# The third block product of the MLP's second matmul as seven inner products, and the order of the products around it

## The chip, the cores and the metric

The kernel runs on one core of a Trainium2 chip. The metric is the device time of one execution, in microseconds (us). The engines are TensorE (PE, with PEld for its weight loads), VectorE (DVE), ScalarE (ACT), GpSimd (POOL) and SyncE (SP), which issues most of the loads.

## The reference

One layer of a transformer-like block on 1024 tokens of width 1024. The part that matters here is the end of it, the MLP with a squared ReLU, and the gated residual behind it:

```python
def _sq_relu_mlp(h, w1, w2):
    return jnp.square(jax.nn.relu(h @ w1)) @ w2

y_x = _sq_relu_mlp(_modulate(x, g_pre_mlp[l], sh2, sc2), w_mlp_in[l], w_mlp_out[l])
x = x + gt2 * _rmsnorm(y_x, g_post_mlp[l])
```

`w1` is 1024 x 4096 and `w2` is 4096 x 1024, all in float32. The second product is therefore (1024 x 4096) times (4096 x 1024).

## The kernel before

**Precision.** Every large matrix is split in a high part `h` (rounded, by ACT, line 169) and a low part `l` (what is left, by DVE, line 175). One float32 product is three matmuls: high times high, high times low, low times high (`three`, lines 221 to 223). A matmul takes 128 x 128 weights and up to 512 columns, and adds into one of eight PSUM banks of 512 columns.

**Seven products instead of eight.** The second product is cut into 2 x 2 blocks (512 tokens, 2048 of the inner dimension, 512 columns) and is computed in the way of Strassen and Winograd, with seven block products P1 to P7 and sums of blocks. The left blocks are the hidden values A11, A12, A22 and their sums S1 to S4, which the first product leaves in DRAM (`hidd`; `keep`, line 1876). The right blocks are columns of `w2` (b11, b12, b21, b22), with the differences t1, t2, t3, t4 made on DVE (`operands`, lines 2037 to 2061). Banks named `pyx`, `pyy`, `pyv` and `pyz`, four each (one for every 128 tokens), take the sums. P1 and P2 go into x (the first block of the result). P6 + P1 gives u2. P7 + u2 goes into the row halves of tokens 512 to 1023, with P5 added, then P4 into v, and P3 and P5 into z.

**Groups.** A product has eight groups (`NG`). A group is 256 of the inner dimension: four banks, each with two steps of three matmuls, so 24 matmuls of 512 columns. The order of the groups is written out by hand in `items`:

- P1, eight groups
- P6 and P2 alternating, then P7 and P5 alternating
- P4 and P3 alternating for four groups, then P3's last four, then P4's last four

`prepare` takes the next item of that list: it issues its loads on SP, its differences and low parts on DVE and its high parts on ACT. It is called ahead of each group, for the item three places on (`AHEAD`). The order of instructions on PE, ACT, DVE and SP is the order of the program in this part (`in_order`), so that an instruction which waits holds up all that are behind it on its engine. Buffers also set the pace: `wraw` has four raw pages (loads of `w2`), `h` four pages (loads of hidden values), `whl` four pairs of high and low parts, and the common pool 33 pages. The weights' high part of an item can only be written when the group four places before has left its pair.

**The tail.** P3's last two groups and P4's last four are computed bank by bank, so that a bank of 128 tokens is done early. Behind each finished bank come the row steps. `gated` takes the mean square on ACT (line 154) and multiplies by the gate on DVE (line 2154). `rsqrt_of` forms the sum of both halves on DVE (line 161) and the root on POOL (line 163). `end` adds the residual (`xo`, line 2162) and stores the row tile. The last 128 tokens are computed in two halves of 256 columns (banks `pyv` and `pyw`). Before the last four groups of P4, DVE adds u2 into the banks v (line 2231).

In the loop of P4 and P3 the four row halves of tokens 512 to 1023 get P5 (`s5`, copied out of z by ACT), are squared and are gated:

```python
c = half(4 + g, 1)
nc.vector.tensor_tensor(c, c, s5[g], add)
gated(4 + g, 1, c)
```

Of the kernel before, what the change touches and what calls it, by code (L numbers as in the profile page):

```python
# [18 lines left out]
P = 128  # L19
# [84 lines left out]
def hybrid_block(ctx, tc, x, ctx_in, w_mod, mod_pages, w_u, b_mod, gp1, gp2, w_in, pool_w, rpb, w_out, w1, w2, vectors,  # L104
# [17 lines left out]
    def page(name, dt=F32):  # L122
        return act.tile([P, 1024], dt, tag="pg", name=name)
# [145 lines left out]
    def mod_gate(name, acc, g, bank):  # L269
        nc.vector.tensor_tensor(acc[:, :256], mod_sums_of(name, acc, bank), g, mul)  # L270
# [1248 lines left out]
    with tc.tile_pool(name="ps2", bufs=6, space=PSUM) as ps2:  # L1519

      def bank(name):
          if name[:3] == "phv" or name in ("poz_0", "poz_1") or name[:2] in ("px", "py") and name[-2:] in ("_3", "_7"):
              return lasting(name)
          return ps2.tile([P, 512], F32, tag="mm", name=name)

      with ExitStack() as tmp2:
# [257 lines left out]
        def second_steps(b12, b22):  # L1784
# [13 lines left out]
            for name in ("T2", "T1", "T3", "B22", "T4"):  # L1798
# [6 lines left out]
        EARLY, SPILLED = 10, 6  # L1805

        hidd = {n: [dram.tile([P, 1024], F32, tag=f"hd{n}_{g}", name=f"hd{n}_{g}") for g in range(NPAIR // 2)]
                for n in ("A11", "A12", "A22", "S1", "S2", "S3", "S4")}

        s1d = [dram.tile([P, 512], F32, tag=f"s1_{p}", name=f"s1_{p}") for p in range(SPILLED)]  # L1810

# [44 lines left out]
            nc.scalar.activation(r, r, AF.Square)  # L1856

        def kept(name, p):
            return hidd[name][p // 2][:, (p % 2) * 512 : (p % 2) * 512 + 512]


# [149 lines left out]


        w2v = w2.rearrange("(k i p) n -> i p k n", i=2, p=P)
        t1, t2 = {}, {}
# [5 lines left out]
        def wcols(name, i, h, g):  # L2020
            return columns(wraw.tile([P, 1024], F32, tag="raw", name=f"{name}_{g}"), i, h, g)
# [6 lines left out]
        def hidden(name, g, early=False):  # L2028
            if early:
                r = wraw.tile([P, 1024], F32, tag="raw", name=f"hr{name}_{g}")  # L2030
            else:
                r = tmp.tile([P, 1024], F32, tag="h", name=f"hr{name}_{g}", bufs=4)
            nc.sync.dma_start(r, hidd[name][g])
            return split_pages(f"hh{name}_{g}", r)


        def operands(name, g, made=None):
            made = made or high_low
            if name == "P1":
                t1[g] = columns(page(f"b11_{g}"), 0, 0, g)  # L2040
                return hidden("A11", g, g <= AHEAD + 1), made(f"b11_{g}", t1[g])
            if name == "P2":
                return hidden("A12", g), made(f"b21_{g}", wcols("b21", 1, 0, g))
            if name == "P6":

                b12, b22 = wcols("b12", 0, 1, g), wcols("b22", 1, 1, g)
                nc.vector.tensor_tensor(t1[g], b12, t1[g], sub)
                t2[g] = page(f"t2_{g}")
                nc.vector.tensor_tensor(t2[g], b22, t1[g], sub)
                return hidden("S2", g), made(f"t2_{g}", t2[g])  # L2050
            if name == "P5":
                return hidden("S1", g), made(f"t1_{g}", t1[g])
            if name == "P7":
                b12, b22 = wcols("b12", 0, 1, g), wcols("b22", 1, 1, g)
                nc.vector.tensor_tensor(b12, b22, b12, sub)
# [4 lines left out]
            nc.vector.tensor_tensor(b21, b21, t2[g], sub)  # L2060
# [54 lines left out]
        with tc.issue_after(first[ET.PE]), in_order(ET.PE, ET.Activation, ET.DVE, ET.SP):  # L2115
# [5 lines left out]
            def four(name):  # L2121
                return [bank(f"{name}_{t}") for t in range(4)]
# [24 lines left out]
            def half(m, h):  # L2147
                return rows[m][:, h * 512 : (h + 1) * 512]
# [31 lines left out]


            pg = bank("pgb")
            x = four("pyx")
            for g in range(NG):
                if g == 1:
                    gain = mod_gain(gp2, page("gpb")[:, :256], nc.gpsimd)
                if g == 3:
                    mod_gate("b", acc_b[-1], gain, lambda name: pg)
                    mod_out("b", acc_b[-1])
                group(x, "P1", g)  # L2190
            s1 = halves("s1")
            for t in range(4):
                nc.scalar.copy(s1[t], x[t])
            y = four("pyy")
            for g in range(NG):
                group(y, "P6", g)
                if g == NG // 2:
                    G2 = gate_page("b")
                if g == NG - 1:
                    u2 = halves("u2")  # L2200
                    for t in range(4):
                        nc.vector.tensor_tensor(u2[t], y[t], s1[t], add)
                group(x, "P2", g, more=True)
            for t in range(4):
                rows[t] = page(f"row{t}")
                gated(t, 0, x[t])
            v, z = four("pyv"), four("pyz")
            for g in range(NG):
                group(v, "P7", g)
                if g == NG - 1:  # L2210
                    for t in range(4):
                        rows[4 + t] = page(f"row{4 + t}")
                        nc.vector.tensor_tensor(half(4 + t, 1), v[t], u2[t], add)
                group(z, "P5", g)
            s5 = halves("s5")
            for t in range(4):
                nc.scalar.copy(s5[t], z[t])
            for g in range(NG // 2):
                group(v, "P4", g, more=True, last=(g == NG // 2 - 1))
                group(z, "P3", g, more=True)  # L2220
                c = half(4 + g, 1)
                nc.vector.tensor_tensor(c, c, s5[g], add)
                gated(4 + g, 1, c)
            for g in range(NG // 2, NG - 2):
                group(z, "P3", g, more=True)
            while coming:
                prepare()

# [71 lines left out]
```

## Time and profile before

| what | value |
|---|---|
| median of 3 runs | 1021.81 us (1021.76 to 1022.08) |
| profiled execution: span from first to last instruction | 1019.4 us |
| mean granted clock of TensorE | 0.998 |
| busy over the span | PE 99%, DVE 73%, ACT 54%, POOL 15% |
| first matmul of the second product | 707.8 us |
| last matmul | 1013.42 us |

The profile gives the span of its execution, and no time of it beside that; the median of the runs is 2.4 us longer. Times within the profile are us from the start of the span. A row in order of time reads: start, length, engine, line, operation, what is written from what is read, and in brackets how long the engine had been idle and what it had waited for. Names leave out buffer numbers, so that the four banks of `pyv` all read `pyv`. Matmuls are pipelined: the distance from one start to the next is their rate, and their length is not.

### The profile page before, as it was taken

What the parts mean: (1) busy time and instruction counts of PE and PEld (TensorE: products, weight loads), DVE (VectorE), ACT (ScalarE), POOL (GpSimd) and SP (SyncE); (2) the same over time, 40 slices, a digit from 0 to 9 for tenths busy, and PEclk for the clock granted to TensorE, in tenths of its full rate; (3) what the DMA queues carried; (4) which work ended last, traced back from release to release, by engine and by line L of the source; (5) the groups of instructions that cost most, each with busy time, mean ns of one, the idle gap of its engine ahead of it and who ended that gap; (6) DMA issues with size and microseconds to landing.
All of it is one profiled execution on the core that took longest, in us unless ns stands there. A gap on an engine that the chain in (4) does not pass through costs nothing.

```text
span 1019.4 us, 16277 instructions
## 1 busy us (share of the span) xinstructions
PE 1008.7 (99%) x6010; PEld 834.4 (82%) x6010; DVE 746.4 (73%) x1170; ACT 548.1 (54%) x964; POOL 154.5 (15%) x234
## 2 busy tenths in 40 slices
PE   8999999999999999999999999999999999999997
PEld 5788888878998888888888888888888888888886
DVE  5588767977885689879988888745757666557576
ACT  6672254348986746786555544555543343334442
POOL 4111210166774221410000000000000000000002
PEclk9999999999999999999999999999999999999999
DMA  9899798641448945885776657537967766556555
GB/s 368 314 295 305 256 265 293 206 104 43 96 95 204 232 183 187 297 216 197 256 260 208 213 194 225 177 135 251 347 218 261 248 228 214 200 167 203 169 184 226
DMA packets 117312, 222.72 MB, mean 218 GB/s; under 512 B 9521, under 2 KB 47281, under 8 KB 117233
## 3 DMA queue, kind: packets, MB, share of 16 engines
q1 hardware_dynamic: 90736, 171.14, 50.0%
q0 software_dynamic: 9360, 19.58, 9.3%
q10 hardware_dynamic: 17136, 30.97, 8.1%
q8 instruction: 47, 0.77, 0.3%
q14 instruction: 33, 0.26, 0.1%
HBM read 168.16 MB, written 52.45 MB: 216 GB/s over the span
## 4 chain that ended last, share of the span: by engine, by line
PE 96%; DMA 2%; DVE 1%; ACT 0%; issue 0%; SPq 0%; DVEq 0%; ACTq 0%
PE pu L476 4%; PE pa L1288 4%; PE S L1208 3%; PE phx L221 3%; PE phz L221 3%; PE phv L221 3%; PE pyx L221 3%; PE phx L223 3%; PE phx L222 3%; PE phv L223 3%; PE pyx L222 3%; PE pyz L221 3%; PE phz L223 3%; PE phv L222 3%; PE phz L222 3%; PE pyz L222 3%
## 5 line engine op out<-in xcount | busy, mean ns | idle before, releaser
L1234 ACT ACTIVATE sp<-sp,nm 128x640 f32<-128x640 f32 (+1 forms) x64 | 51.4, 802 | 10.9 <-DVE ri L1238 5.1
L1223 DVE CUSTOM_DVE_ANT_0 sp<-S,tab 128x640 f32<-128x640 f32 (+1 forms) x56 | 44.5, 795 | 13.9 <-PE pz L1254 9.5
L1855 ACT ACTIVATE c<-c 128x512 f32<-128x512 f32 x48 | 30.3, 632 | 44.8 <-DVE c L1975 25.6
L169 ACT CAST wpS<-S 128x512 fp32r<-128x512 f32 x64 | 38.7, 616 | 27.4 <-PE phv L223 9.7
L221 PE MATMUL phx<-thB,wpA 128*128 128x512 f32 x128 | 50.2, 392 | 0.0
L222 PE MATMUL phx<-tlB,wpA 128*128 128x512 f32 x128 | 49.8, 389 | 0.0
L223 PE MATMUL phx<-thB,wpA 128*128 128x512 f32 x128 | 49.8, 389 | 0.0
L175 DVE TENSOR_TENSOR wpS<-S,wpS 128x512 fp32r<-128x512 f32 x64 | 43.5, 688 | 7.6 <-ACT wpS L169 7.5
L163 POOL TENSOR_TENSOR ry<-vy,nhalf 128x1 f32<-128x1 f32 x7 | 5.4, 767 | 275.6 <-DVE vy L161 275.6
L1856 ACT ACTIVATE c<-c 128x512 f32<-128x512 f32 x48 | 30.3, 631 | 15.1 <-DVE sa L1938 12.1
L221 PEld LDWEIGHTS phx<-thB,wpA 128*128 128x128 f32 x128 | 24.0, 188 | 5.5 <-ACT s L1906 0.4
L223 PEld LDWEIGHTS phx<-thB,wpA 128*128 128x128 f32 x128 | 24.0, 188 | 5.0
L222 PEld LDWEIGHTS phx<-tlB,wpA 128*128 128x128 f32 x128 | 24.0, 188 | 4.9
L1273 DVE COPY pt<-T 128x512 f32<-128x512 f32 x32 | 22.0, 687 | 5.5 <-PE T L1254 5.5
L1288 PE MATMUL pa<-pt,v 128*64 128x128 f32 x352 | 25.9, 279 | 0.2
L221 PE MATMUL phv<-thT,wpA 128*128 128x512 f32 x64 | 25.0, 391 | 0.0
L221 PE MATMUL phz<-thB,wpS 128*128 128x512 f32 x64 | 25.0, 391 | 0.0
L223 PE MATMUL phv<-thT,wpA 128*128 128x512 f32 x64 | 24.9, 389 | 0.0
L222 PE MATMUL phz<-tlB,wpS 128*128 128x512 f32 x64 | 24.9, 389 | 0.0
L222 PE MATMUL phv<-tlT,wpA 128*128 128x512 f32 x64 | 24.9, 389 | 0.0
L221 PE MATMUL phy<-thT,wpS 128*128 128x512 f32 x64 | 24.9, 389 | 0.0
L222 PE MATMUL phy<-tlT,wpS 128*128 128x512 f32 x64 | 24.9, 389 | 0.0
(1179 smaller groups left out, 3442.6 us busy)
## 6 DMA issues: line engine op xcount, KB each, us to landing
b<-in_w SPq DMA_DIRECT2D x64, 512.0 KB, 4.3
hrS<-hdS SPq DMA_DIRECT2D x32, 512.0 KB, 5.1
hrA<-hdA SPq DMA_DIRECT2D x24, 512.0 KB, 5.6
wm<-in_mod_pages SPq DMA_DIRECT2D x16, 512.0 KB, 9.3
wa_0w<-in_w SPq DMA_DIRECT2D x16, 512.0 KB, 5.0
wa_1w<-in_w SPq DMA_DIRECT2D x16, 512.0 KB, 4.3
hdA<-c ACTq DMA_DIRECT2D x32, 256.0 KB, 2.2
hdS<-sa ACTq DMA_DIRECT2D x32, 256.0 KB, 2.2
```

What stands on the lines that cost most here:

```text
L169: nc.scalar.copy(hi, src)
L175: nc.vector.tensor_tensor(lo, src, hi.bitcast(F32), sub)
L221: nc.tensor.matmul(ps, ahi, bhi, start=first, stop=False, skip_group_check=more)
L222: nc.tensor.matmul(ps, ahi, blo, start=False, stop=False, skip_group_check=more)
L223: nc.tensor.matmul(ps, alo, bhi, start=False, stop=last, skip_group_check=more)
L476: nc.tensor.matmul(pus[b][j], wk(wgt, k, low, j * P, P), r, start=(k == 0 and n == 0), stop=(k == KT - 1 and n == 2))
L1208: nc.tensor.matmul(S[e][:, c0 : c0 + k[0].shape[1]], q[n_q][hs, cols], k[n_k][hs], start=(n_q + n_k == 0), stop=(n_q == 1))
L1223: nc.vector.tensor_tensor_reduce(out=to, in0=s, in1=bt, scale=1.0, scalar=BIG, op0=add, op1=ALU.min, accum_out=nm)
L1234: nc.scalar.activation(sp, sp, AF.Exp, bias=least[i, e], scale=-1.0, accum_out=sums[i][:, e : e + 1])
L1288: nc.tensor.matmul(pa[e * HD : (e + 1) * HD, cols], v[:, f : f + HD], turns[i][:, e, c] if c < 4 else fifths[i][:, :, (e + 1) * HD : (e + ...
L1855: nc.scalar.activation(r, src, AF.Relu)
L1856: nc.scalar.activation(r, r, AF.Square)
```

## The change

P3 (S4 times b22) is itself cut into 2 x 2 blocks and computed with seven inner products M1 to M7 of 256 tokens, 1024 of the inner dimension and 256 columns. Each has two halves (h = 0, 1) of 24 matmuls of 256 columns. One half stands ahead of each group of P1 (from the fifth) and P2 (two ahead of P2's first and fifth). S4 is kept in a tensor of its own, `hidq`, from which pieces of 256 columns are loaded. The inner sums are read from banks `pyi...`, which alternate between the two lasting banks, and are put together in four pages; those that hold the result get u2 in the loop of P4 and P5, and are added in the tail (`u4`) in the place of u2.

The order of the other products becomes: P1 and P2 with the inner ones, P6 with P7, P4 with P5, P5's last four, P4's last four. P7 takes t3 from P6's preparation and loads nothing of `w2`. P4 makes t2 anew from b22 and t1, with one more load and one more subtraction. P5 goes into z alone, so that the row halves of tokens 512 to 1023 get it in the tail.

```diff
-          if name[:3] == "phv" or name in ("poz_0", "poz_1") or name[:2] in ("px", "py") and name[-2:] in ("_3", "_7"):
+          if (name[:3] in ("phv", "pyi") or name in ("poz_0", "poz_1") or name[:2] == "px" and name[-2:] in ("_3", "_7")
+                  or name in ("pyy_3", "pyv_3", "pyz_3")):
               return lasting(name)
...
+        hidq = [dram.tile([P, 4, 1024], F32, tag=f"hq{h}", name=f"hq{h}") for h in range(2)]
...
             if name == "P6":
                 b12, b22 = wcols("b12", 0, 1, g), wcols("b22", 1, 1, g)
                 nc.vector.tensor_tensor(t1[g], b12, t1[g], sub)
-                t2[g] = page(f"t2_{g}")
-                nc.vector.tensor_tensor(t2[g], b22, t1[g], sub)
+                nc.vector.tensor_tensor(b12, b22, b12, sub)
+                t3[g] = b12
+                nc.vector.tensor_tensor(b22, b22, t1[g], sub)
...
             if name == "P7":
-                b12, b22 = wcols("b12", 0, 1, g), wcols("b22", 1, 1, g)
-                nc.vector.tensor_tensor(b12, b22, b12, sub)
-                return hidden("S3", g), made(f"t3_{g}", b12)
+                return hidden("S3", g), made(f"t3_{g}", t3.pop(g))
-            if name == "P3":
-                return hidden("S4", g), made(f"b22_{g}", wcols("b22", 1, 1, g))
-            b21 = wcols("b21", 1, 0, g)
-            nc.vector.tensor_tensor(b21, b21, t2[g], sub)
+            b22, b21 = wcols("b22", 1, 1, g), wcols("b21", 1, 0, g)
+            nc.vector.tensor_tensor(b22, b22, t1[g], sub)
+            nc.vector.tensor_tensor(b21, b21, b22, sub)
             return hidden("A22", g), made(f"t4_{g}", b21)
...
+        INNER = ("M1", "M5", "M6", "M4", "M2", "M3", "M7")
+        def inner_operands(name, h):
+            a = lambda r, c, at=None: inner_raw(f"a{r}{c}{name}_{h}", True, r, c, h, at)
+            b = lambda r, c, at=None: inner_raw(f"b{r}{c}{name}_{h}", False, r, c, h, at)
+            new = lambda n: kept_raw.setdefault((n, h), page(f"{n}i_{h}"))
+            if name == "M1":
+                x, y = a(0, 0, new("S")), b(0, 0, new("T"))
+            elif name == "M5":
+                x, more, y, less = a(1, 0, new("S1")), a(1, 1), kept_raw["T", h], b(0, 1)
+                combine(x, x, more, add)
+                combine(y, less, y, sub)
...
+            else:
+                x, z, y, less = a(0, 0), a(1, 0), b(1, 1), b(0, 1)
+                combine(x, x, z, sub)
+                combine(y, y, less, sub)
+            return split_pages(f"hh{name}_{h}", x), high_low(f"w{name}_{h}", y)
...
-        items = [("P1", g) for g in range(NG)]
-        for a, b in (("P6", "P2"), ("P7", "P5")):
-            items += [(n, g) for g in range(NG) for n in (a, b)]
-        items += [(n, g) for g in range(NG // 2) for n in ("P4", "P3")] + [("P3", g) for g in range(NG // 2, NG)]
+        inner = iter([(n, h) for n in INNER for h in range(2)])
+        items = [("P1", g) for g in range(4)]
+        for n in [("P1", g) for g in range(4, NG)] + [("P2", g) for g in range(NG)]:
+            items += [*islice(inner, 2 if n in (("P2", 0), ("P2", 4)) else 1), n]
+        items += [(n, g) for g in range(NG) for n in ("P6", "P7")]
+        items += [(n, g) for g in range(NG // 2) for n in ("P4", "P5")] + [("P5", g) for g in range(NG // 2, NG)]
         items += [("P4", g) for g in range(NG // 2, NG)]
...
+            def inner_group(name, h):
+                prepare()
+                a, w = made.pop((name, h))
+                if h == 0:
+                    inner_banks[name] = bank(f"pyi{name}")
+                ps = inner_banks[name]
+                for t in range(2):
+                    for j in range(4):
+                        ts, cs = slice(j * 256 + t * P, j * 256 + (t + 1) * P), slice(j * 256, (j + 1) * 256)
+                        three(ps[:, t * 256 : (t + 1) * 256], a[0][:, ts], a[1][:, ts], w[0][:, cs], w[1][:, cs],
+                              h + t + j == 0, h == 1 and j == 3, more=t > 0)
+                if h == 1:
+                    inner_kept(name, ps)
...
+                group(v, "P7", g)
             for t in range(4):
+                rows[4 + t] = page(f"row{4 + t}")
+                nc.vector.tensor_tensor(half(4 + t, 1), v[t], u2[t], add)
+            z = four("pyz")
+            u4 = [inner_part(f"c{t // 2}")[:, t % 2 * 512 : t % 2 * 512 + 512] for t in range(4)]
             for g in range(NG // 2):
                 group(v, "P4", g, more=True, last=(g == NG // 2 - 1))
-                group(z, "P3", g, more=True)
-                c = half(4 + g, 1)
-                nc.vector.tensor_tensor(c, c, s5[g], add)
-                gated(4 + g, 1, c)
+                group(z, "P5", g)
+                nc.vector.tensor_tensor(u4[g], u4[g], u2[g], add)
...
             for t in range(4):
-                token_sums(z, t, [made["P3", g] for g in (NG - 2, NG - 1)], False, True, True)
-                finish(t, 1, z[t], xts[t], u2[t])
+                token_sums(z, t, [made["P5", g] for g in (NG - 2, NG - 1)], False, True, False)
+                c = half(4 + t, 1)
+                nc.vector.tensor_tensor(c, c, z[t], add)
+                gated(4 + t, 1, c)
+                finish(t, 1, z[t], xts[t], u4[t])
```

More of the change, by code (lines that the diff above doesn't have):

```diff
@@ L2047, in operands @@
                 nc.vector.tensor_tensor(t1[g], b12, t1[g], sub)
-                t2[g] = page(f"t2_{g}")
-                nc.vector.tensor_tensor(t2[g], b22, t1[g], sub)
-                return hidden("S2", g), made(f"t2_{g}", t2[g])
+                nc.vector.tensor_tensor(b12, b22, b12, sub)
+                t3[g] = b12
+                nc.vector.tensor_tensor(b22, b22, t1[g], sub)
+                return hidden("S2", g), made(f"t2_{g}", b22)
             if name == "P5":
@@ L2182, in hybrid_block @@
             pg = bank("pgb")
-            x = four("pyx")
[L2184 to L2191, printed above, removed]
+            inner_banks, parts = {}, {}
+            by_two = lambda v: v.rearrange("p (t n) -> p t n", t=2)
@@ new lines, in hybrid_block @@
+            x = four("pyx")
+            for name, g in items[: items.index(("P6", 0))]:
+                if name in INNER:
+                    inner_group(name, g)
+                elif name == "P1":
+                    if g == 1:
+                        gain = mod_gain(gp2, page("gpb")[:, :256], nc.gpsimd)
+                    if g == 3:
+                        mod_gate("b", acc_b[-1], gain, lambda name: pg)
+                        mod_out("b", acc_b[-1])
+                    group(x, "P1", g)
+                    if g == NG - 1:
+                        s1 = halves("s1")
+                        for t in range(4):
+                            nc.scalar.copy(s1[t], x[t])
+                else:
+                    group(x, "P2", g, more=True)
+                    if g == NG // 2:
+                        G2 = gate_page("b")
@@ L2192, in hybrid_block @@
             for t in range(4):
-                nc.scalar.copy(s1[t], x[t])
-            y = four("pyy")
+                rows[t] = page(f"row{t}")
+                gated(t, 0, x[t])
+            y, v = four("pyy"), four("pyv")
             for g in range(NG):
                 group(y, "P6", g)
-                if g == NG // 2:
-                    G2 = gate_page("b")
                 if g == NG - 1:
```

69 lines of the change are left out of this document (52 added, 17 removed).

## The prediction, made before the changed kernel was run

> **What bounds the kernel now.** I read the page first, then a table of the stages of the second MLP product, then single instructions in order of time on TensorE and VectorE.
>
> ```profile
> span 1019.4 us, 16277 instructions
> PE 1008.7 (99%) x6010; PEld 834.4 (82%) x6010; DVE 746.4 (73%) x1170; ACT 548.1 (54%) x964; POOL 154.5 (15%) x234
> ...
> 751.90:838.90 87.00, 87.00 (x385) 72.06 (x384) 57.67 (x52) 34.38 (x39) 0.00 (x0) 1.00 0.71 240
> 926.00:969.50 43.50, 43.50 (x194) 36.02 (x193) 27.12 (x27) 20.29 (x26) 0.00 (x0) 1.00 0.65 205
> 969.50:991.25 21.75, 21.75 (x98) 18.01 (x97) 17.26 (x17) 9.05 (x9) 0.00 (x0) 1.00 0.44 150
> 991.25:1013.70 22.45, 22.45 (x122) 19.40 (x120) 17.58 (x30) 6.81 (x18) 5.37 (x7) 1.00 0.70 278
> 1013.70:1019.40 5.70, 0.00 (x0) 0.00 (x0) 2.04 (x5) 0.77 (x3) 0.00 (x0) 0.69 0.26 92
> ```
>
> The columns of the stages are the stretch, its length, and the busy time of PE, PEld, DVE, ACT and POOL. TensorE (PE) is busy without a gap to 1013.7, at a granted clock of 1.00. So before 1013.7 a saving counts only if it takes time from PE, and new work elsewhere counts only if PE, or the end, comes to wait for it. VectorE (DVE) is the second engine: 79% busy at 969.5 to 991.25 and 78% in the last PE stage. That is where I looked for the price.
>
> **Part 1, the matmuls.** The third product was 8 groups of 24 matmuls of 512 columns, 192 in all. The seven inner ones take 7 x 2 halves x 24 = 336 matmuls of 256 columns. Both kinds stand in the last PE stage:
>
> ```profile
> 991.47 0.39 PE L221 MATMUL pyv<-t_4h,hhA_4h 128*128 128x512 f32 x1
> ...
> 1007.56 0.39 PE L223 MATMUL pyv<-t_7h,hhA_7l 128*128 128x512 f32 x1
> ...
> 1007.79 0.28 PE L221 MATMUL pyv<-t_4h,hhA_4h 128*128 128x256 f32 x1
> 1007.79 0.19 PEld L222 LDWEIGHTS pyv<-t_4l,hhA_4h 128*128 128x128 f32 x1
> ...
> 1013.42 0.28 PE L223 MATMUL pyw<-t_7h,hhA_7l 128*128 128x256 f32 x1
> ```
>
> The first pair of rows spans 72 matmuls of 512 columns: 16.09 us over 71 steps, 0.2266 each (the 0.39 is a pipelined length, not a rate). The second spans 48 of 256 columns: 5.63 over 47 steps, 0.1198 each. So 192 x 0.2266 = 43.51 goes and 336 x 0.1198 = 40.25 comes: **-3.26 us**, not the eighth (5.4) that the columns alone promise. A group of 512 lasts 24 x 0.2266 = 5.44, an inner half 2.88.
>
> The Trainium skill (TensorE: Matmul & The Clock Gate, Back-to-back issue gap) gives an isolated step of N/2.4 + 2.5 ns, so 215.8 and 109.2 ns, and the sum by it, an estimate, would be -4.8 us. The rows here are 5% and 10% slower than that, and the measured steps are kept.
>
> **Part 2, feeding the inner stage: nothing.** From the fifth group of P1 to the last of P2 lie 12 groups and 14 inner halves: 65.3 + 40.3 = 105.6 us of PE. DVE owes 26 items two low parts each (1.14 from one start to the next, rows below), 16 combinations of 1024 columns (M5 2, M6 2, M4 1, M3 1, M7 2, for both halves) at 1.25, and 7 half pages of sums at 0.60: 59.3 + 20 + 4.2 = 83.5, 79%. Items are prepared three ahead, at least 2.88 + 5.44 + 2.88 = 11.2 us before use, and an item with two combinations needs 4.8. If that cover fails, PE stops for what DVE or a load is late (rival 3). Loads: 124 of 512 KB for 120 in the whole second product (inner 28, P4 +8, P3 -16, P7 -16). All go in order on SP's queue, and pieces of 1 KB a partition have a nearest row of their own (w1's pages), beside 2 KB pieces:
>
> ```profile
> b<-in_w SPq DMA_DIRECT2D x64, 512.0 KB, 4.3
> wa_0w<-in_w SPq DMA_DIRECT2D x16, 512.0 KB, 5.0
> GB/s 368 314 295 305 256 265 293 206 104 43 96 95 204 232 183 187 297 216 197 256 260 208 213 194 225 177 135 251 347 218 261 248 228 214 200 167 203 169 184 226
> ```
>
> A landing 0.7 us later is hidden in that lead. Cost at 0; ends 0 and +4.6 (rival 3). Two inner sums share the pair of PSUM banks, and each is read out by ACT or DVE while the inner product on the other bank runs (5.8): 0. The fourth P1 sum's move to the six other banks, the stores of S4 (same pieces, other tensor) and P6/P7 (8.3 of 10.9 us on DVE for a pair of groups: three subtractions and four low parts) are 0 for the same cover.
>
> **Part 3, P4 straight behind P7.** Before, P5's last group lay between P7's last group and P4's first; now P4 adds to the very banks that DVE must read first (v + u2). The like place before is P6's end:
>
> ```profile
> 732.55 1.22 DVE L2047 TENSOR_TENSOR b<-b,b 128x1024 f32<-128x1024 f32 x1
> 733.80 1.22 DVE L2049 TENSOR_TENSOR t<-b,b 128x1024 f32<-128x1024 f32 x1
> ...
> 833.48 0.39 PE L223 MATMUL pyy<-t_7h,hhS_7l 128*128 128x512 f32 x1
> ...
> 833.91 0.69 DVE L2202 TENSOR_TENSOR u<-pyy,s 128x512 f32<-128x512 f32 x1 [0.67 <-PE pyy L223]
> 834.52 1.22 DVE L2055 TENSOR_TENSOR b<-b,b 128x1024 f32<-128x1024 f32 x1
> 835.65 1.22 DVE L175 TENSOR_TENSOR hhS_1l<-hrS,hhS_1h 128x1024 fp32r<-128x1024 f32 x1
> 836.90 1.23 DVE L175 TENSOR_TENSOR t_1l<-b,t_1h 128x1024 fp32r<-128x1024 f32 x1
> 838.04 1.88 DVE L2154 TENSOR_TENSOR row<-pyx,Gb 128x512 f32<-128x512 f32 x3
> ```
>
> P6's group ends at 833.48 + 0.23 = 833.71, and DVE then does u2's last quarter, one subtraction, two low parts, and reaches the next sum at 838.04. P4's preparation has two dependent subtractions (1.25 by the first two rows), so the first v + u2 starts at about 839.24 and ends at 839.93; PE wants that bank at 833.71 + 5.44 = 839.15. **+0.8 us** on PE; ends 0 (the preparation is ahead) and +2. Below 0 is excluded here and in part 2: PE has no gap in these stages that could close.
>
> **Part 4, the tail.** The fourth product now subtracts twice per group. P5's end, which sets the row halves of tokens 4 to 7, now comes last: their add, square and gate leave the P4/P3 loop and stand in the tail, once per tile, on DVE's queue ahead of everything that finishes rows.
>
> ```profile
> 933.87 0.69 DVE L2222 TENSOR_TENSOR row<-row,s 128x512 f32<-128x512 f32 x1
> 935.35 0.69 DVE L2154 TENSOR_TENSOR row<-row,Gb 128x512 f32<-128x512 f32 x1 [0.79 <-ACT jy L154]
> ...
> 981.69 1.23 DVE L175 TENSOR_TENSOR t_5l<-b,t_5h 128x1024 fp32r<-128x1024 f32 x1 [1.99 <-ACT t_5h L169]
> 982.83 1.22 DVE L2060 TENSOR_TENSOR b<-b,t 128x1024 f32<-128x1024 f32 x1
> ...
> 986.32 1.22 DVE L2060 TENSOR_TENSOR b<-b,t 128x1024 f32<-128x1024 f32 x1
> ...
> 989.80 2.22 DVE L2231 TENSOR_TENSOR pyv<-pyv,u 128x512 f32<-128x512 f32 x4
> 991.92 0.68 DVE L2176 TENSOR_TENSOR c<-pyz,u 128x512 f32<-128x512 f32 x1
> ...
> 993.53 0.68 DVE L2154 TENSOR_TENSOR row<-c,Gb 128x512 f32<-128x512 f32 x1
> 994.13 0.68 DVE L2176 TENSOR_TENSOR c<-pyz,u 128x512 f32<-128x512 f32 x1
> ...
> 1002.39 1.28 DVE L2162 SCALAR_TENSOR_TENSOR xo<-row,ry,xo 128x1024 f32<-128x1024 f32 x1 [0.44 <-POOL ry L163]
> ...
> 1004.47 1.28 DVE L2162 SCALAR_TENSOR_TENSOR xo<-row,ry,xo 128x1024 f32<-128x1024 f32 x1
> ...
> 1009.65 1.28 DVE L2162 SCALAR_TENSOR_TENSOR xo<-row,ry,xo 128x1024 f32<-128x1024 f32 x1
> ...
> 1011.37 0.43 DVE L2171 TENSOR_TENSOR row<-pyv,Gb 128x256 f32<-128x256 f32 x1 [0.43 <-ACT jy L154]
> ...
> 1014.83 1.54 DVE L2266 SCALAR_TENSOR_TENSOR xo<-row,inverse_y,xo 128x512 f32<-128x512 f32 x3
> ```
>
> Step by step, on the times of before. (a) The second subtraction of P4's groups 4 and 5 falls into waits (the 1.99 at 981.69). Groups 6 and 7 follow back to back (982.83, 986.32), so each adds 1.25: v + u2 starts 2.5 late, at 992.3. PE wants its first bank at 991.47 and stands about 1.6, which does not decide. (b) DVE reaches the first tile at 991.92 + 2.5 = 994.42. From 991.92 to the fourth finished row (1002.39) lay 10.47 us for four tiles, with next to no idle. Each tile now adds a sum, which waits out ACT's square before it may be overwritten (933.87 to 935.35: 1.48), and a gate of 0.60 (993.53 to 994.13): 2.08, four times 8.3. The fourth row is at 994.42 + 18.8 = 1013.2. (c) The next three rows take 2.08 each (1002.39 to 1004.47): the seventh, 1009.65 before, is at 1019.4. (d) Then the last tile's first quarter (+1.2), the small sum (+0.35), second quarter, root and reciprocal (+0.6) and three pieces of 1.54: end at 1023.2, where it was 1014.83 + 1.54 = 1016.37. PE's last matmul, at 1013.42 + 1.6, no longer ends it. **+6.8 us.** Removed in exchange: the same four sums and gates from the loop and four ACT copies, all under PE time: 0. Ends: +4.3 (a costs nothing) and +8 (the reciprocal roots on POOL, on which each row waits, take longer).
>
> **Sum.** -3.26 + 0.8 + 6.8 = +4.4 us against the span: 1019.4 to 1023.8. The median of the runs is 1021.81, 2.4 above the span, and I carry that over: **1026.2 us**, 0.4% slower. About 0.2% (2 us) is what a measurement of this kernel can tell from no change.
>
> **Rivals.** (1) *The tail's new DVE work is hidden*, and PE stays the end: 1021.81 - 3.26 + 0.8 = 1019.4. For it: in the two stages from 991.25 DVE has 4.9 and 3.7 us idle, together about the 8.3 that is added. Against it: DVE's idle time lies after 1007.8, behind the rows, and 3.7 of it after PE's end. It decides if the chain from 991.92 to the last row grows by under 2.5 us; I count 6.8, so 4.4 would have to be wrong. Chance 0.13. (2) *The tail starts on time*: P4's preparations run far enough ahead that (a) is nothing: 1026.2 - 2.5 = 1023.7, no change. For it: the waits of almost 2 us ahead of two low parts. Against it: the last two have none. 0.10. (3) *The inner stage starves*: M7 needs 4 loads a half beside 2 for each group, 6 x 0.524 MB in 8.32 us, 378 GB/s, where the page's best slice is 368 and the best late one 347. Two such rounds at 297 GB/s would take 21.2 us instead of 16.6: up to +4.6, so 1028 to 1031. Against it: the halves of M2 and M3 ahead load one page each, and buffers take loads early. 0.12. (4) *Weight loads set the inner step*: at the 0.19 of a load, 336 x 0.188 = 63.2 us, 1026.2 + 22.9 = 1049. Against it: the 48 matmuls after 1007.79 step at 0.12 with loads of 0.19 beside them. 0.03. The Trainium skill (TensorE: Matmul & The Clock Gate, The mechanism) says that weight loads overlap matmuls in flight only when the row group differs, which speaks for (4); the trace shows overlap with full 128 x 128 weights, so here it does not hold.
>
> **How the numbers follow.** The forecast has 0.62 and a range of its own of 1024.6 (half of (a) hidden and nothing at P4: -1.25 - 0.8, with the slack of a few tenths) to 1028.5 (+2 at P4 and the tail's upper end of +8). With (2) and (3) that is 0.84 between 1022 and 1030.5, which is the range; left out are (1) and (4). Faster 0.13 is (1), within 0.2% 0.10 is (2), slower 0.77 the rest.
>
> **What would show it.** Right: inner matmuls stepping at 0.12 and no PE gap from P1 to P7; a gap near 0.8 ahead of P4's first matmul; a gap near 1.6 ahead of the last product's second half; DVE at nearly full from there to the end, PE's last matmul 8 us ahead of DVE's last instruction (3 before). Wrong: PE's last matmul followed by the final row within 3 us (1), the first row's sum at its old distance from P5's end (2), PE gaps before inner matmuls (3), steps of 0.19 (4).

## The result, and the profile after

The changed kernel takes **1027.44 us** (median of 5 runs, 1027.31 to 1027.78) beside 1021.89 for the kernel before on the same chip (5 runs, 1021.76 to 1022.08): a ratio of 1.0055 [1.0043, 1.0067], 5.55 us slower. On a second chip it was 1.0055 [1.0041, 1.0069]. The forecast was 1026.2, 4.4 slower.

First the head of the changed kernel's page with its fourth view (the engine shares of the chain of work that ended last, followed back from the last instruction), then that view of the kernel before, then the stages of the second MLP product, with the columns that the prediction explained.

```profile
span 1025.5 us, 16659 instructions
PE 1006.3 (98%) x6154; PEld 838.3 (82%) x6154; DVE 795.2 (78%) x1217; ACT 559.4 (55%) x974; POOL 154.6 (15%) x234
...
DVE 0%; POOLq 0%; DVEq 0%; ACT 0%; issue 0%; ACTq 0%
```

```profile
PE 96%; DMA 2%; DVE 1%; ACT 0%; issue 0%; SPq 0%; DVEq 0%; ACTq 0%
```

```profile
751.90:836.58 84.68, 84.68 (x499) 75.38 (x497) 70.64 (x65) 43.32 (x47) 0.00 (x0) 1.00 0.74 252
836.58:924.84 88.26, 87.44 (x386) 71.86 (x384) 71.66 (x66) 36.94 (x44) 0.00 (x0) 1.00 0.57 198
...
968.48:990.24 21.76, 21.76 (x97) 17.84 (x95) 19.16 (x17) 9.24 (x9) 0.00 (x0) 1.00 0.56 198
990.24:1014.12 23.88, 22.35 (x121) 19.33 (x120) 19.28 (x32) 9.23 (x26) 4.20 (x5) 1.00 0.50 195
1014.12:1025.50 11.38, 0.16 (x2) 0.00 (x0) 7.64 (x14) 0.92 (x5) 1.17 (x3) 0.71 0.59 230
```

PE is no longer in the chain that ends the program, as far as the view follows it: the shares are near 0 because it goes back only over the last 4.6 us, and the rows of DVE below show what lies ahead of that. The stretch behind PE's last matmul has grown from 5.7 to 11.4 us. P1 to P2 with the inner products (the first row, most of it) run without a gap in PE although DVE is 83% busy there; in the last 21.8 us before P5's end DVE is 88% busy, where it was 79%.

PE has two waits in the whole of the second product, and had none before. The view of waits of the changed kernel, for PE from 705 us on (engine, line that waits, releaser: total, times, longest):

```profile
PE pyv L221 <- DVE pyv L2319: 1.5, 1, 1.5
PE pyv L221 <- DVE row L2305: 0.8, 1, 0.8
```

PE in order of time: the first inner half (24 matmuls), the first matmul behind it, then the two gaps.

```profile
730.74 0.28 PE L221 MATMUL pyiM<-wM_0h,hhM_0h 128*128 128x256 f32 x1
...
733.49 0.28 PE L223 MATMUL pyiM<-wM_0h,hhM_0l 128*128 128x256 f32 x1
733.61 0.40 PE L221 MATMUL pyx<-b_4h,hhA_4h 128*128 128x512 f32 x1
...
923.63 0.39 PE L223 MATMUL pyv<-t_7h,hhS_7l 128*128 128x512 f32 x1
924.84 0.47 PE L221 MATMUL pyv<-t_0h,hhA_0h 128*128 128x512 f32 x1 [0.82 <-DVE row L2305]
...
990.01 0.39 PE L223 MATMUL pyz<-t_7h,hhS_7l 128*128 128x512 f32 x1
991.93 0.47 PE L221 MATMUL pyv<-t_4h,hhA_4h 128*128 128x512 f32 x1 [1.53 <-DVE pyv L2319]
```

And DVE in order of time, from the preparation of P4's last group to the end. These answer to the rows that the prediction showed of 986.32 to 1014.83.

```profile
986.35 1.22 DVE L2063 TENSOR_TENSOR b<-b,b 128x1024 f32<-128x1024 f32 x1
987.60 1.23 DVE L2064 TENSOR_TENSOR b<-b,b 128x1024 f32<-128x1024 f32 x1
988.74 1.22 DVE L175 TENSOR_TENSOR hhA_7l<-hrA,hhA_7h 128x1024 fp32r<-128x1024 f32 x1
989.95 1.23 DVE L175 TENSOR_TENSOR t_7l<-b,t_7h 128x1024 fp32r<-128x1024 f32 x1
991.09 2.22 DVE L2319 TENSOR_TENSOR pyv<-pyv,u 128x512 f32<-128x512 f32 x4
993.22 0.68 DVE L2330 TENSOR_TENSOR row<-row,pyz 128x512 f32<-128x512 f32 x1
994.68 0.69 DVE L2200 TENSOR_TENSOR row<-row,Gb 128x512 f32<-128x512 f32 x1 [0.79 <-ACT jy L154]
995.29 0.69 DVE L2222 TENSOR_TENSOR c<-pyz,c0i 128x512 f32<-128x512 f32 x1
...
1012.14 1.29 DVE L2208 SCALAR_TENSOR_TENSOR xo<-row,ry,xo 128x1024 f32<-128x1024 f32 x1 [0.44 <-POOL ry L163]
...
1018.39 1.28 DVE L2208 SCALAR_TENSOR_TENSOR xo<-row,ry,xo 128x1024 f32<-128x1024 f32 x1
...
1020.70 1.54 DVE L2357 SCALAR_TENSOR_TENSOR xo<-row,inverse_y,xo 128x512 f32<-128x512 f32 x3
```

Three stretches add up to the difference. They are cut at the first matmul of the second product (707.79 before, 708.18 after), at P5's end on the z banks (the last matmul's start and one step, 990.01 + 0.23 = 990.24; before, where P3 came last on z, the next matmul's start, 991.47), at the start of v + u2 (989.80 and 991.09) and at DVE's last end (1016.37 and 1022.24):

| stretch | before | after | difference |
|---|---|---|---|
| first matmul to the end on z | 283.68 | 282.06 | -1.62 |
| from there to the start of v + u2 | -1.67 | +0.85 | +2.52 |
| v + u2 to the end of DVE's last instruction | 26.57 | 31.15 | +4.58 |
| sum | 308.58 | 314.06 | +5.48 |

PE gains 1.6 us up to the z end, and DVE gives back 7.1 behind it.

### The profile page after: what moved, and what is told of

It is laid out like the page before. It is cut to its first block, busy times and chain, and to the rows that moved or that the text cites. A ratio compares the mean times of both kernels' runs of the same rounds, so it can differ in the third digit from the quotient of the medians.

```text
span 1025.5 us, 16659 instructions
## 1 busy us (share of the span) xinstructions
PE 1006.3 (98%) x6154; PEld 838.3 (82%) x6154; DVE 795.2 (78%) x1217; ACT 559.4 (55%) x974; POOL 154.6 (15%) x234
## 5 line engine op out<-in xcount | busy, mean ns | idle before, releaser
L221 PE MATMUL phz<-thB,wpS 128*128 128x512 f32 x64 | 25.0, 391 | 0.0
L223 PE MATMUL phz<-thB,wpS 128*128 128x512 f32 x64 | 24.9, 389 | 0.0
```

The source lines that it names most:

```text
L221: nc.tensor.matmul(ps, ahi, bhi, start=first, stop=False, skip_group_check=more)
L223: nc.tensor.matmul(ps, alo, bhi, start=False, stop=last, skip_group_check=more)
```

## The experiments

A is the changed kernel. A time "below A" goes by the runs of the kernel before on the chip of the run, with A put 5.6 us above them. A itself was measured on two chips and gave 5.6 on both; for the runs on other chips this figure is taken over. **T** is the prediction's theory: DVE's chain behind P5's end is what ends the program; it starts late because of P4's second subtraction, and is longer by four sums and gates. The rivals: **R1**, PE's own two waits are the loss; **R2**, the inner stage loses it; **R3**, the gap ahead of P4 is absorbed later; **R4**, work moved to POOL is not free for DVE; **L**, loads are what is late next. In the traces I compare **the stretch** from the first matmul of the second product to DVE's last end (314.1 in A), since the start of the second product moves by some tenths from run to run; it needs no other run on the same chip.

**A once more, on another chip.**

> The changed kernel itself, unchanged, as the measure for the runs beside it on the same chip (A below). Between chips the kernel before differed by 0.7 us (1021.9 and 1021.2). Expected 5.5 us above before.

Measured: 1026.68 (1026.58 to 1027.15) beside 1021.07, the stretch 314.18. It is the yardstick for what follows.

**The row halves' gates back in the loop, without P5 in them.** The edit takes the four sums out, so that these row halves lack P5, and puts squares and gates where P4 and P5 alternate:

```diff
                 nc.vector.tensor_tensor(u4[g], u4[g], u2[g], add)
+                gated(4 + g, 1, half(4 + g, 1))
...
-                c = half(4 + t, 1)
-                nc.vector.tensor_tensor(c, c, z[t], add)
-                gated(4 + t, 1, c)
```

> Leaves P5 out of the row halves of tokens 512 to 1023: their squares and gates stand in the loop of P4 and P5 again, and the tail has the old steps, with P4's second subtraction kept. T: DVE has 8.3 us less behind P5, more than its lead over PE, so that PE's last matmul (1014.0 in the trace of after, with its wait of 1.5) ends the program as it did before, 2.95 us ahead of the last row and 6 us ahead of the end: span 1020.0 instead of 1025.5, time about 1022. R1: PE's waits are unchanged, 1027.4. R2: 1027.4.

Measured: 1021.60 (11 runs), 1.0005 [0.9996, 1.0014]; the stretch is 308.78, **5.3 shorter than A's**. PE's two waits are what they were in A (0.8 and 1.5), and the inner stage is untouched, so neither R1 nor R2 can be the cause. DVE's chain with the last quarter:

```profile
1012.39 0.15 DVE L2346 SCALAR_TENSOR_TENSOR rest_y<-sy,sy 128x1 f32<-128x1 f32 x1
1014.98 0.42 DVE L2217 TENSOR_TENSOR row<-pyw,Gb 128x256 f32<-128x256 f32 x1 [2.44 <-ACT jy L154]
```

DVE now stands 2.44 us for the last quarter's square, that is for PE: PE ends the program again. Of the 8.3 us of row steps taken out, 5.3 show in the stretch, since PE's end then binds.

**P4's first subtraction left out of groups 4 to 7.** The loads stay; t4 is another matrix in these groups.

```diff
             b22, b21 = wcols("b22", 1, 1, g), wcols("b21", 1, 0, g)
-            nc.vector.tensor_tensor(b22, b22, t1[g], sub)
+            if g < 4:
+                nc.vector.tensor_tensor(b22, b22, t1[g], sub)
```

> Leaves out the first of P4's two subtractions for groups 4 to 7 (the loads stay), so that t4 is another matrix. Theory T (the chain on DVE from P5's end ends the program): DVE's sum v + u2 starts 2.5 us earlier, and the whole chain behind it with it: 1027.4 - 2.5 = 1024.9. Rival R1 (PE's waits for DVE are the loss, and the row steps would fit behind PE): only PE's wait of 1.5 us ahead of the last product's second half goes: 1025.9. Rival R2 (the loss lies ahead of the tail, in the inner stage): no change, 1027.4.

Measured: 1025.88 (1025.76 to 1026.38), 1.0045 [1.0031, 1.0059]; the stretch is 312.99: **1.1 shorter, where T said 2.5** (0.9 by the medians). PE's wait ahead of the late half fell from 1.5 to 0.5, by about as much as the time, so this run doesn't tell T from R1. DVE in order of time shows why less than half of it came:

```profile
985.01 1.22 DVE L2065 TENSOR_TENSOR b<-b,b 128x1024 f32<-128x1024 f32 x1 [0.30 <-DMA b<-in_w]
987.35 1.23 DVE L175 TENSOR_TENSOR hhA_7l<-hrA,hhA_7h 128x1024 fp32r<-128x1024 f32 x1 [1.11 <-ACT hhA_7h L169]
```

The next bound is the loads. The last group's page of `w2` is 0.30 late and its hidden page, for which ACT's rounding waits, 1.1: together the 1.4 that is missing. P4 loads two pages of `w2` per group, where it loaded one. Why they are late stands in the same run's rows of DVE, SP and ACT:

```profile
980.00 1.23 DVE L175 TENSOR_TENSOR t_5l<-b,t_5h 128x1024 fp32r<-128x1024 f32 x1 [1.94 <-ACT t_5h L169]
981.26 0.37 SPq L2021 DMA_DIRECT2D b<-in_w  x1
...
986.27 1.05 ACT L169 CAST hhA_7h<-hrA 128x1024 fp32r<-128x1024 f32 x1 [2.81 <-DMA hrA<-hdA]
```

SP issues the last load of `w2` at 981.26, 0.03 behind the end of DVE's low part `t_5l` (981.23), the last instruction that reads the raw page which this load takes over: with four raw pages and two loads per group, a page comes free only two groups later. The hidden page's load stands behind it on SP (981.67).

**The same, with the hidden page's load issued ahead of the two others.**

```diff
+            r = tmp.tile([P, 1024], F32, tag="h", name=f"hrA22_{g}", bufs=4)
+            nc.sync.dma_start(r, hidd["A22"][g])
             b22, b21 = wcols("b22", 1, 1, g), wcols("b21", 1, 0, g)
...
-            return hidden("A22", g), made(f"t4_{g}", b21)
+            return split_pages(f"hhA22_{g}", r), made(f"t4_{g}", b21)
```

> As the run with one subtraction in P4's groups 4 to 7 (the same part is left out), with one thing more: in P4's preparation the load of the hidden page is issued ahead of the two loads of w2 on SP. Without that, the sum v + u2 came only 1.05 us earlier than in after, instead of 2.5, and the trace showed ACT and DVE waiting for the last hidden page, whose load stood on SP behind a load that waited for a raw page. Theory L (that queueing was the next bound): the sum comes 2.2 us earlier than in after, 2.2 below A. Rival (the raw page itself, four for two loads a group, is the bound): 1.1 below A, as without the reorder.

Measured: 1025.28 (1024.35 to 1025.5), 1.0038 [1.0025, 1.005], 1.4 below A and between the two expectations (1.1 and 2.2); the stretch is 312.51, 1.6 shorter. The hidden page is on time, and the page of `w2` takes over as the late one:

```profile
985.57 1.22 DVE L2067 TENSOR_TENSOR b<-b,b 128x1024 f32<-128x1024 f32 x1 [0.92 <-DMA b<-in_w]
```

v + u2 starts 1.6 earlier than A's, measured from P5's end. The order of the loads on SP was a part of what is late (0.5), and the page of `w2` is the rest: its load still goes out only at 981.20, 0.02 behind the low part `t_5l`. So L holds, and the rival that the raw page is the bound holds beside it. PE's wait ahead of the late half is gone, 1.5 us, so the time alone would fit R1 too; the next experiment parts them.

**The second load taken away too: t2 kept.** Groups 4 to 7 keep the t2 that P6 makes, in pages of the common pool, so that P4 has one subtraction and one load less there. The whole computation stays.

```diff
-                nc.vector.tensor_tensor(b22, b22, t1[g], sub)
-                return hidden("S2", g), made(f"t2_{g}", b22)
+                to = b22 if g < 4 else t2.setdefault(g, page(f"t2_{g}"))
+                nc.vector.tensor_tensor(to, b22, t1[g], sub)
+                return hidden("S2", g), made(f"t2_{g}", to)
...
+                b22, b21 = t2.pop(g), wcols("b21", 1, 0, g)
```

> t2 of groups 4 to 7 is kept in pages from P6's preparation (as before the change, for these four), so that P4's groups 4 to 7 make one subtraction and load one page less. The computation is whole. T with L (subtraction and load queue together made the 2.5 us): the sum v + u2 comes 2.5 us earlier as predicted, 2.5 below A, where leaving out the subtraction alone gave 1.05 in the trace and putting the hidden page's load first 1.6. Rival: something else holds the preparation (ACT, the pairs of high and low parts): 1.5 below A again.

Measured: 1023.94 (1023.5 to 1024.99), 1.0029 [1.0017, 1.004], **2.8 below A**. DVE in order of time:

```profile
985.18 1.22 DVE L175 TENSOR_TENSOR hhA_7l<-hrA,hhA_7h 128x1024 fp32r<-128x1024 f32 x1
986.39 1.22 DVE L175 TENSOR_TENSOR t_7l<-b,t_7h 128x1024 fp32r<-128x1024 f32 x1
987.53 2.22 DVE L2323 TENSOR_TENSOR pyv<-pyv,u 128x512 f32<-128x512 f32 x4
```

v + u2 starts 1.72 ahead of P5's end (989.25), as it did before the change (1.67). PE's wait ahead of the late half is gone as in the run above, but the time is lower still, by 1.4 in the medians and by 1.05 in the stretch (311.46, 2.6 shorter than A's): it follows v + u2 and not PE's wait, T and not R1. Subtraction and load together are worth the 2.5 that the prediction gave the subtraction; without the subtraction but with the load, only 1.1 of it comes.

**Both subtraction and gates out.** The edits of the second and third experiments together, with what they leave out.

> Both: one subtraction in P4's groups 4 to 7, and the gates in the loop without P5. This leaves what the change does to PE ahead of the tail. T: no wait of PE ahead of the last half, PE ends: about 1022 - 1.6 = 1020.5, which is 1.4 below before (the PE gain of 3.26 less 1.1 at P4's start, 0.2 at P6's start and 0.4 in the groups beside inner halves). R1: 1027.4 - 1.5 = 1025.9. R2: 1027.4.

Measured: 1020.61 (11 runs), 0.9994 [0.9985, 1.0002]: 0.6 below the kernel before, and no clear gain, where 1.4 was expected. The stretch of the profiled execution, the slowest of the 11, is 308.06, 0.5 below; its second product begins 1.1 us later than A's, which the stretch leaves out. What is missing is PE's: 0.8 us remain of the wait ahead of the late half, because of the late load, beside the 0.8 at P4. With the tail's work gone, PE ends the program and its waits count.

**P5 ahead of P4 in the alternation.** P4's first group then has a group of P5 between it and P7's last, as before the change. The whole computation stays.

```diff
-        items += [(n, g) for g in range(NG // 2) for n in ("P4", "P5")] + [("P5", g) for g in range(NG // 2, NG)]
+        items += [(n, g) for g in range(NG // 2) for n in ("P5", "P4")] + [("P5", g) for g in range(NG // 2, NG)]
...
-                group(v, "P4", g, more=True, last=(g == NG // 2 - 1))
                 group(z, "P5", g)
+                group(v, "P4", g, more=True, last=(g == NG // 2 - 1))
```

> P5 and P4 alternate with P5 first, so that a group of P5 lies between P7's last group and P4's first again. The computation is whole. T: the gap of PE ahead of P4 (0.8 to 1.1 us) closes, and as the tail's chain starts from P5's end on PE, the whole tail comes earlier: 1026.4. Rival R3 (DVE is the bound all the way through P4 and P5, so that PE's gap is free): 1027.4.

Measured: 1025.84 (1025.5 to 1026.3), 1.0043 [1.0031, 1.0056]; the stretch is 313.21, **0.9 shorter** (1.0 by the medians). The gap of 0.8 is gone and its 0.9 came through to the end: R3 falls. A delay of PE ahead of P5's end moves DVE's tail as a whole.

**The four new gates on POOL.** The whole computation stays.

```diff
-                nc.vector.tensor_tensor(half(m, h), src, G2[:, h * 512 : (h + 1) * 512], mul)
+                (on or nc.vector).tensor_tensor(half(m, h), src, G2[:, h * 512 : (h + 1) * 512], mul)
...
-                gated(4 + t, 1, c)
+                gated(4 + t, 1, c, on=nc.gpsimd)
```

> The four new gates (row halves of tokens 512 to 1023 times the gate) go from DVE to POOL; the sums stay on DVE. The computation is whole. T: DVE loses, per tile, the wait for ACT's square and the gate, 1.48 us, so 5.9 in all; then PE's last matmul ends the program: 5.2 below A, and PE still waits 1.5 ahead of the last half. Rival R4 (POOL, at 1.29 us for a 128x512 product of two tensors elsewhere in the trace, delays the roots that each row waits for, or slows DVE): 2 to 3.5 below A.

Measured: 1024.46 (1024.25 to 1024.6), 1.0032 [1.002, 1.0045], **2.2 below A where T said 5.2**. PE's waits are unchanged. POOL's and then DVE's rows in order of time:

```profile
994.02 1.29 POOL L2200 TENSOR_TENSOR row<-row,Gb 128x512 f32<-128x512 f32 x1 [266.77 <-ACT jy L154]
997.42 2.05 POOL L2200 TENSOR_TENSOR row<-row,Gb 128x512 f32<-128x512 f32 x1 [1.07 <-ACT jy L154]
```

```profile
997.05 1.27 DVE L2208 SCALAR_TENSOR_TENSOR xo<-row,ry,xo 128x1024 f32<-128x1024 f32 x1
998.26 1.23 DVE L161 SCALAR_TENSOR_TENSOR vy<-sy,sy 128x1 f32<-128x1 f32 x1
```

POOL's product takes 1.29 when it starts while DVE is idle and 2.05 when it starts while DVE has a row in work (997.05 to 998.32). And DVE's sum of two single columns, 0.16 elsewhere, takes 1.23 and ends at 999.49, when POOL's product does (999.47). Each waits for the other to finish. The four sums of this kind take 0.74, 1.23, 1.24 and 1.24, in all 3.8 more than in A; of the 5.9 that T takes from DVE, 2.1 is left, beside the 2.2 measured: R4. The Trainium skill (SBUF — State Buffer, SBUF: two separate sides) says that DVE and GpSimd share one pair of ports, taken as an exclusive lock for a whole instruction, and that a DVE instruction with two SBUF inputs contends for it with a GpSimd instruction that reads SBUF; these rows agree, with the two ends 0.02 apart.

**P5 first, the load first, the gates and P4's late first subtractions on POOL.** The whole computation stays; beside the edits above:

```diff
-            nc.vector.tensor_tensor(b22, b22, t1[g], sub)
+            (nc.gpsimd if g >= 4 else nc.vector).tensor_tensor(b22, b22, t1[g], sub)
```

> All mendings together, with the computation whole: P5 ahead of P4 in the alternation, the four gates on POOL, the first of P4's subtractions on POOL for groups 4 to 7, and the hidden page's load first. T: PE has no wait from P1 to its last matmul but some tenths at P6's start, and ends the program: 5.2 + 1.5 + 0.9 = 7.6 below A, so 2 below before. R4: POOL's subtractions (about 2.6 us each) come late or hold DVE up, 5 below A, no better than before.

Measured: 1023.29 (11 runs, 1022.77 to 1024.23), 1.0022 [1.0013, 1.0031], **3.4 below A where T said 7.6**. It is hardly more than the sum of the order (0.9) and the gates (2.2). POOL's, then DVE's rows:

```profile
960.57 2.41 POOL L2065 TENSOR_TENSOR b<-b,b 128x1024 f32<-128x1024 f32 x1 [3.98 <-DMA b<-in_w]
...
981.44 3.17 POOL L2065 TENSOR_TENSOR b<-b,b 128x1024 f32<-128x1024 f32 x1 [4.84 <-DMA b<-in_w]
```

```profile
982.33 3.37 DVE L175 TENSOR_TENSOR t_6l<-b,t_6h 128x1024 fp32r<-128x1024 f32 x1
```

The low part of 1.23 takes 3.37: it stands until POOL's subtraction ends (984.61), then does its own 1.1. In that group POOL spared DVE 1.2 and held it for 2.1; and the shortest of POOL's subtractions takes twice DVE's time for one (2.41 beside 1.22).

**The sum in a tile of its own.** The sum of row half and P5 no longer overwrites what ACT is squaring, so the gate needn't wait for the square. Nothing goes to POOL; the whole computation stays.

```diff
-                c = half(4 + t, 1)
-                nc.vector.tensor_tensor(c, c, z[t], add)
+                c = tmp.tile([P, 512], F32, tag="c", name=f"ch{t}", bufs=1)
+                nc.vector.tensor_tensor(c, half(4 + t, 1), z[t], add)
```

> A below is the changed kernel: 5.6 us above before on either chip. Edit: the new sum of half and P5 goes into a tile of its own instead of back into the row half, so that DVE's gate need not wait for ACT's square of the same data; it stays on DVE. The computation is whole. T: 0.79 to 0.85 us of wait per tile goes, four times: 3.3 below A. Rival R5 (the gates' work itself, not the wait, is what counts, or the sum of squares is then the next wait): 1 below A.

Measured: 1023.50 (11 runs), 1.0022 [1.0013, 1.003], **3.2 below A**. DVE in order of time:

```profile
992.74 0.67 DVE L2330 TENSOR_TENSOR ch<-row,pyz 128x512 f32<-128x512 f32 x1
993.45 0.69 DVE L2200 TENSOR_TENSOR row<-ch,Gb 128x512 f32<-128x512 f32 x1
```

The gate follows the sum without the 0.79 that A's row at 994.68 shows; the four such waits of A, 0.79 to 0.85, made 3.3. R5 falls. Of the prediction's 2.08 per tile, 0.8 was an avoidable wait.

**v + u2 one group behind P4's fourth**, that is, four groups earlier, out of the tail. The whole computation stays.

```diff
+                if g == NG // 2:
+                    for t in range(4):
+                        cs = slice(0, 512 if t < 3 else 256)
+                        nc.vector.tensor_tensor(v[t][:, cs], v[t][:, cs], u2[t][:, cs], add)
...
-            for t in range(4):
-                cs = slice(0, 512 if t < 3 else 256)
-                nc.vector.tensor_tensor(v[t][:, cs], v[t][:, cs], u2[t][:, cs], add)
```

> The four sums v + u2 ahead of P4's last four groups are done one group after P4's fourth, between DVE's waits there, instead of behind all of the preparation. The computation is whole. T: the 2.1 us of these sums leave the chain from the last preparation to the last row (the row steps start at 991.1 instead of 993.2 of after's trace): 2.1 below A, though PE's wait is only 1.5. R1 (PE's waits are the loss): 1.5 below A.

Measured: 1026.02 with a wide spread (1025.08 to 1027.53), 1.0051 [1.0038, 1.0065]: 0.7 below A in the medians, 1.3 to 1.5 in the traces (a stretch of 312.73 for 314.06 and 314.18). The size stays open: T's 2.1 is not met, and the traces alone can't exclude R1's 1.5. DVE in order of time:

```profile
970.23 2.22 DVE L2317 TENSOR_TENSOR pyv<-pyv,u 128x512 f32<-128x512 f32 x4
...
990.31 1.23 DVE L175 TENSOR_TENSOR t_7l<-b,t_7h 128x1024 fp32r<-128x1024 f32 x1
991.45 0.68 DVE L2331 TENSOR_TENSOR row<-row,pyz 128x512 f32<-128x512 f32 x1
```

From 970.23 to 991.45 DVE has no idle time: the 2.1 us of sums found waits of DVE for only 1.3 of them. The last low part, which in A starts 0.29 ahead of P5's end, starts 0.52 behind it (989.79), and the row steps start 1.66 behind it where A's start 2.98 behind it.

**All that worked, and nothing on POOL.** P5 first, t2 kept, the sum in its own tile, v + u2 early: the four edits above together. The whole computation stays.

> The three mendings above together, and P5 ahead of P4 in the alternation; nothing on POOL, as POOL's products of two tensors held DVE's instructions up for their whole length in the runs before. The computation is whole. T: DVE's chain is shorter than PE's, PE has no wait but some tenths at P6's start, and ends the program: PE's 3.26 less 0.4 (groups beside inner halves) and 0.5 (P6's start): 2.2 to 2.4 below before. If the chain on DVE still ends it (3.3 + 2.1 + 2.5 + 0.9 below A): 3.2 below before is its bound, so PE decides. R1 or R5: no better than before.

Measured: **1018.41** (1017.95 to 1018.74) beside 1021.12, 0.9974 [0.9963, 0.9984]: 2.7 below the kernel before and 8.3 below A. PE has no wait in the second product. The four edits brought 0.9, 2.8, 3.2 and 0.7 alone, 7.6; with a subtraction per group fewer in groups 4 to 7, DVE has waits for the early sums to fill. ACT's and DVE's last rows in order of time:

```profile
1010.56 0.38 ACT L154 ACTIVATE jy<-pyw 128x256 f32<-128x256 f32 x1 [2.46 <-PE pyw L223]
...
1011.07 0.42 DVE L2221 TENSOR_TENSOR row<-pyw,Gb 128x256 f32<-128x256 f32 x1 [0.87 <-ACT jy L154]
...
1011.60 1.54 DVE L2362 SCALAR_TENSOR_TENSOR xo<-row,inverse_y,xo 128x512 f32<-128x512 f32 x3
```

ACT waits 2.46 for PE's last bank, and the end follows 3 us behind PE's last matmul, as in the kernel before. What is left of the change is then its first part: the stretch is 305.84, 2.74 below the kernel before, beside the 3.26 that the matmuls spare; the rest is the slower groups beside the inner halves (0.36) and at P6's start (0.2).

## Why the prediction was right

The change is slower by 5.55 where 4.4 was forecast, and for the reasons that were given: PE gains, and DVE's longer and later tail takes more than that. Point by point:

- **Part 1, the matmuls (-3.26).** Right. The first inner half takes 2.75 us over 23 steps, 0.1196 each, with a weight load of 0.19 beside each; all 14 halves take 2.87 to 2.88. Rival (4) fell with them. What the sum lacked: the 12 groups of 512 columns beside an inner half take 5.47, not 5.44 (the first matmul behind one is 0.40 long and followed after 0.24), 0.36 in all.
- **Part 2, feeding the inner stage (0).** Right: no gap in PE from P1 to P2. DVE was busy 89.3 of the 105.8 us of this stage (84%) for the 79% worked out, which left out six subtractions of P6's preparation, 7.3 us, that run ahead into it. Rival (3) fell. One term was wrong by 0.23: P6's first group takes 5.67. Its third bank starts at 839.38, just behind the first of the four gates that read `pyx` (line 2200, 838.64, 0.69 long); in the run with P5 first the view of waits puts 0.2 us of PE down to that line.
- **Part 3, P4 behind P7 (+0.8).** The wait measured 0.8; the slower first groups around it make it 1.1, and the experiment with P5 first got 0.9 back.
- **Part 4 (a), v + u2 2.5 late.** Right in size, 2.52, and half in cause: taking out the subtraction alone gives back 1.1, because the second load per group, which part 2 put among the hidden ones, is late by 1.4 behind it. PE's stand of "about 1.6" was 1.5 (1.7 to the next start), and did not decide.
- **Part 4 (b) to (d).** From the first tile's step to the fourth row, 18.9 (993.22 to 1012.14) for 18.8; to the seventh row 6.25 for 6.2; to the end 3.85 for 3.8. The whole tail from v + u2 on grew by 4.58 for 4.3 (992.3 to 1023.2 against 26.57 before). PE's last matmul stands 8.2 us ahead of DVE's last end, as foretold. Rivals (1) and (2) fell by these rows.
- **The sum.** Span 1025.5 for 1023.8. The profiled execution took 1027.31 by itself, 1.8 above its span; in the recorded runs of the kernel before it is 1.7 to 2.1. So the 2.4 carried over, from a median and the span of one execution, was about 0.6 too much and hid part of the 1.7 by which the span was too short: that part is luck. The 1.7 is, but for rounding, 0.36 + 0.23 + 0.3 at P4 + 0.3 in the tail, 0.4 by which the second product began later (708.18 for 707.79; 707.54 in the second profile of the same kernel), and 0.2 behind DVE's last instruction.

## What to carry to other kernels

Before an arithmetic saving on the busy engine is counted, list which instructions the new order puts behind the last common point (here P5's end) on the engine that finishes the work, and walk that queue instruction by instruction: here 3.3 us of matmuls were paid for with 8.3 us of row steps that had been free, and with a start of these steps 2.5 us later. In such a queue look first for waits that a tile of its own removes (3.2 us here by one edit), then for operands that can be kept instead of made anew (2.8); and after every step taken out, ask which load is late next. Work moved from DVE to POOL while DVE is busy is not off DVE's path, unless its rows show that the two don't hold each other.

## What the runs showed of the hardware that was not expected

- A product of two tensors on POOL (128 x 512, 1.29 us when it starts while DVE is idle) takes 2.05 when it starts while DVE is at work, and then holds DVE's next instruction until it ends: an instruction of 0.16 us took 1.23, one of 1.23 took 3.37 beside a POOL subtraction of 3.17.
- A group of 512-column matmuls right behind one of 256 columns takes 0.03 us longer (5.47 for 5.44, 12 times). Behind a wait of PE of 0.82 the first matmul is 0.47 long and the second follows after 0.30 instead of 0.23; that group takes 5.56. The 0.82 is counted from the modelled end of the matmul ahead; from start to start, PE stood 0.98 longer than a step.
- With the first subtraction of P4's groups 4 to 7 left out, the last page of `w2` came 0.30 late, and 0.92 with the hidden page's load ahead of it. In both runs its load went out 0.02 to 0.03 behind the instruction of DVE that freed its raw page. With one load per group the same load went out at 960.43, some 20 us earlier. So, by these rows, the four raw pages set the time of this load, and the order on SP's queue added the lateness of the hidden page behind it.
